# Key and value compression run as one pass: both halves of the array's columns, copies on ScalarE, sums shared with GpSimd

## The chip, the cores and the metric

The kernel runs on one core of a Trainium2 chip. The metric is the device time of one execution in microseconds (us), as the median of several runs. Engines are named as in the profile: PE (TensorE matmul), PEld (its weight load), DVE (VectorE), ACT (ScalarE), POOL (GpSimd), SP (SyncE, which issues the transfers).

## The reference

The program is a chain of blocks over 256 positions of width 1024: two "hybrid" layers, a gated delta-rule block with a context, and a mixture of 16 experts. The change is in the hybrid layers. Each projects its input to many streams, runs three attention mixers and mixes their results:

```python
h = split_cols(u @ w_in)                    # dq dk iq ik iw | fq fk fv | nq kc vc ks kw ... gate
o_dsa = dsa_mixer(dq, dk, h["dsa_v"], iq, ik, iw)   # top-64 keys by an index score
o_fox = fox_mixer(fq, fk, fv, logf)                 # six heads with a decay
kc = nsa_compress(kvs("nsa_kc"), cmp_pe[0], cmp_w1[0], cmp_w2[0])
vc = nsa_compress(kvs("nsa_vc"), cmp_pe[1], cmp_w1[1], cmp_w2[1])
...
def nsa_compress(kv, pe, w1, w2):           # 15 windows of 32 positions, stride 16, 2 groups of 64
    blocks = kv[:, idx] + pe                # idx: the 32 positions of each window
    return silu(blocks.reshape(..., 32 * 64) @ w1) @ w2
```

The nsa mixer, the third one, attends to the 15 compressed keys and values among others.

## The kernel before, in words

The two hybrid layers are two calls of `layer` (L661). It walks over a list of 17 chunks of the projection: NA, (dk, ik), (iq0, iq1), (dq0, dq1), (kc, vc), (fq0, fk0), NB, (fq1, fk1), and so on. A pair chunk has two halves of 128 columns. To keep fp32 precision, `halves` splits a half's weights into a rounded part `wh`, cast on ACT (L344), and the rest `wl = w - wh` (L345), on DVE or POOL by a pattern `self.pat`: "VVP" sends every third to POOL, "P" every one. `proj_t` then makes eight groups of three matmuls of a half (L433, L434 with `wh`, L435 with `wl`); the first L435 can't start before `wl` is there. NA, NB and NC use `proj_n` (L457) with two splits each. `w` loads of 1 MB are issued on SP.

The result of a half goes on in PSUM: `rope` (copy `rraw` on ACT, a rotation on PE, products on DVE L527 and POOL L528, sum L529) for dk, ik, iq, dq; a plain ACT copy for fq and fk; `compress` (L624) for kc and vc. When iq1 is there `topk` (L808) makes index scores `isc` (PE L819, ACT relu `irel`, DVE sums L829) and finds the 64th largest of each row with eight rounds of MAX8 and MATCH_REPLACE (L845, L846) on DVE, for 256 and for 128 columns, and from it the mask `dmask` (L850). dsa0, dsa1, fox0, ... are calls of `pair` (L532): masks and scores into PSUM on PE (dmask enters by L543, qk by L553), row maxima `nm` on DVE, exponentials on ACT, normalisation, transposes on PE (L592 to L594), PE products into O.

`compress` copies a half from PSUM to K2 (tile `sg`), 64 rows on ACT (L630) and the same shifted by one position into the other 64 rows on DVE (L631), for two groups; makes 16 tiles `cB` of 128x30 with the position's vector added (L634, DVE); multiplies them by `w1` into 64 rows of PSUM, accumulating over 16 (L637; two passes each, so 32 rows of the trace); and applies silu. Its `cB` has one buffer. `cmp_finish` (L872) multiplies by `w2` (L878, L887).

The order of instructions on each engine is not written out by hand: a scheduler orders the whole program when it is built, from dependences and buffers, so small edits move instructions of neighbouring work. In layer 1 a part of the third block, the context's chain, is put in beside the hybrid layer's chunks (`ctx_early`, L1280 to L1516: tiles yT, NB, NC, P, PT), and products of conditioning vectors (L372) fill gaps on PE. After the hybrid layers come the third block and the experts, whose weights (`rw`) stream through a ring of 21 tiles.

Of the kernel before, what the change touches and what calls it, by code (L numbers as in the profile page):

```python
# [186 lines left out]
def prep(inp):  # L187

    f = {k: np.asarray(v) for k, v in inp.items()}
    a = {}  # L190
    a["consts"] = CONST
    x = f["x"][0]
    a["xT"] = x.T.reshape(8, 128, 256).transpose(1, 0, 2)
    a["x"] = x
    a["cT"] = f["c"][0].reshape(8, 128).T

    slabs = lambda w: w.reshape(*w.shape[:-2], 4, 2, 128, 1024).swapaxes(-3, -2).reshape(*w.shape[:-2], 4, 128, 2048)

# [12 lines left out]
    a["cmp_pe"] = pe.reshape(2, 128, 32)
    w1 = f["cmp_w1"].reshape(2, 2, 16, 128, 64).transpose(0, 3, 1, 2, 4)
    a["cmp_w1"] = w1.reshape(2, 128, 2048)
    a["cmp_w2"] = f["cmp_w2"].transpose(0, 2, 1, 3).reshape(2, 64, 128)
    a["w_out"] = slabs(f["w_out"][:, MIX_ROWS, :])
    a["ln_g"] = f["ln_g"]
    a["ln_b"] = f["ln_b"]
    lc = np.stack([f["ln_g"], f["ln_b"]], 1).reshape(2, 2, 8, 128).transpose(0, 3, 1, 2)
    a["ln_col"] = lc.reshape(2, 128, 16)
    g = lambda n: f[n + "_2"]  # L220
    col = lambda v: v.reshape(8, 128).T
    a["c2T"] = np.concatenate([col(g("c")[0]), col(g("c_ctx"))], 1)
# [16 lines left out]
    a["w_gate"] = slabs(g("w_gate")[0])  # L239
    a["w_up"] = slabs(g("w_up")[0])  # L240
    a["w_down"] = slabs(g("w_down")[0][:15])

    a["w_down_last"] = strips(g("w_down")[0][15]).reshape(4, 128, 2, 1024).swapaxes(1, 2)
    a["fin_g"] = g("final_norm_g")[None]
    return {k: np.ascontiguousarray(v) for k, v in a.items()}


class Kern:
# [365 lines left out]
    def compress_consts(self, l):  # L614
        nc = self.nc
        w1 = self.wgtile().rearrange("p (a j o) -> p a j o", a=2, j=16)
        nc.sync.dma_start(w1, self.io["cmp_w1"][l].rearrange("p (a j o) -> p a j o", a=2, j=16))
        pe = self.t([128, 2, 16], "cpe", 2)
        nc.sync.dma_start(pe, self.io["cmp_pe"][l].rearrange("p (a j) -> p a j", a=2))
        w2 = self.t([64, 2, 64], "cw2", 2)  # L620
        nc.sync.dma_start(w2, self.io["cmp_w2"][l].rearrange("p (a o) -> p a o", a=2))
        return w1, pe, w2

    def compress(self, cc, a, p):  # L624

        nc = self.nc
        w1, pe, w2 = cc
        K2 = self.t([128, 2, 256], "sg", 1)
        for g in range(2):
            nc.scalar.copy(K2[0:64, g, :], p[64 * g:64 * g + 64, :])  # L630
            nc.vector.tensor_copy(K2[64:128, g, 0:255], p[64 * g:64 * g + 64, 1:256])  # L631
        B = self.t([128, 16, 2, 15], "cB", 1)
        for j in range(16):
            nc.vector.tensor_scalar(B[:, j], K2[:, :, 2 * j:2 * j + 225:16], pe[:, a, j:j + 1], None, op0=ALU.add)  # L634
        acc = self.psg([64, 2, 15])
        for j in range(16):
            nc.tensor.matmul(acc, w1[:, a, j, :], B[:, j], start=(j == 0), stop=(j == 15))  # L637
# [23 lines left out]
    def layer(self, l, uT, x, m, hook, first=None):  # L661
# [7 lines left out]
        for i, ch in enumerate(CHUNKS):  # L669
            if ch == ("kc", "vc"):  # L670
                cc = self.compress_consts(l)
            hook(i)
            self.pat = "P" if l == 0 and 3 <= i < 6 else "VVP"
            w = self.load_chunk(l, i) if l or i else first
            if isinstance(ch, str):
                N = self.t([128, 2, 256], ch)
                p = self.mmt()
                self.proj_n(p, w, uT)
                nc.vector.tensor_copy(N, p)
                S[ch] = N  # L680
                if ch == "NA":
                    self.after_na(N, bf, S)
                continue
            p = self.mmt()
            for ti, name in enumerate(ch):
                q = p[:, ti, :]
                self.proj_t(q, w[:, :, 128 * ti:128 * ti + 128], uT)
                if name[:2] in ("iq", "ik", "dk", "dq", "ks", "kw"):
                    S[name] = qk()
                    self.rope(S[name], q, 32 if name[0] == "i" else 64)  # L690
                elif name in ("kc", "vc"):
                    S[name] = self.compress(cc, 0 if name == "kc" else 1, q)
                elif name[0] == "g":
                    j = int(name[1])
                    e = self.t([128, 256], "ge", 2)
                    self.sigmoid_big(e, q)
                    nc.vector.tensor_mul(e, e, q)
                    g = S[f"mix{j}"]
                    nc.vector.tensor_mul(g, g, e)
                else:  # L700
                    S[name] = qk()
                    nc.scalar.copy(S[name], q)
                    if name[:2] == "nq":
                        S["r" + name] = qk()
# [1242 lines left out]
```

## Time and profile before

| | us |
|---|---|
| timed runs, median of 3 (lowest to highest) | 1303.93 (1303.80 to 1306.29) |
| the profiled execution's own time | 1295.95 |
| its span in the trace | 1294.2 |
| PE busy | 1048.7 (81%) |
| DVE busy | 558.6 (43%) |
| ACT busy | 387.4 (30%) |
| POOL busy | 264.6 (20%) |
| span of the chain that ended last spent in PE / DMA / DVE / POOL / ACT | 42% / 35% / 11% / 4% / 4% |

The profile lies 1.75 us around its span and 8 us below the timed median. Layer 0 takes about the first 240 us, layer 1 about 300 to 575 us, the experts the stretch from about 850 us on. A row of the timeline gives start, duration, engine, line, operation, what it writes and reads, and in brackets the idle time of its engine before it with what ended it.

### The profile page before, as it was taken

Reading aid. Unit: us, or ns where it says so; the run is one execution under the profiler, and the core shown is the slowest. Engines: PE = TensorE matmul, PEld = TensorE weight load, DVE = VectorE, ACT = ScalarE, POOL = GpSimd, SP = SyncE. Lnnn points to the kernel's source line nnn. Section 1 sums busy time; section 2 is a strip of 40 time slices with the busy share of each in tenths; the row PEclk is TensorE's granted clock in tenths of the full one; section 3 lists DMA queues with packets and bytes.
Section 4 is the critical chain, followed back from the end, with each engine's and each line's share of the span. In section 5 each row is a group of like instructions: output and inputs, shape, how many; then the busy total and the mean of one; then the engine's idle time right before and its main releaser. Section 6 shows DMA issues by size and latency. Waiting matters only on the chain.

```text
span 1294.2 us, 22853 instructions
## 1 busy us (share of the span) xinstructions
PE 1048.7 (81%) x9488; PEld 733.4 (57%) x9488; DVE 558.6 (43%) x1315; ACT 387.4 (30%) x899; POOL 264.6 (20%) x235
## 2 busy tenths in 40 slices
PE   5878999986869999957879999898666766676665
PEld 2766787776757876736778888654322432232232
DVE  2585357777696445586585435620100010010002
ACT  2334337635334425525542434310000000000002
POOL 1431132266421221152424343200000000000000
PEclk9899999999989999977979999899877787787777
DMA  8745864434224385521211555979999999999996
GB/s 357 263 160 204 311 228 171 140 130 176 102 88 168 140 305 191 215 78 39 95 58 40 192 202 215 363 288 417 421 420 419 421 419 420 419 420 420 420 421 247
DMA packets 52569, 330.07 MB, mean 255 GB/s; under 512 B 8049, under 2 KB 9969, under 8 KB 14321
## 3 DMA queue, kind: packets, MB, share of 16 engines
q1 hardware_dynamic: 52464, 328.61, 64.9%
q8 instruction: 74, 1.21, 0.4%
q14 instruction: 31, 0.25, 0.1%
HBM read 327.54 MB, written 1.05 MB: 254 GB/s over the span
## 4 chain that ended last, share of the span: by engine, by line
PE 42%; DMA 35%; DVE 11%; POOL 4%; ACT 4%; issue 4%; POOLq 0%; SPq 0%; DVEq 0%; ACTq 0%
DMA rw<-in_w_up 13%; DMA rw<-in_w_down 11%; DMA rw<-in_w_gate 5%; PE mm L433 4%; PE mm L435 4%; PE mm L434 4%; DMA w<-in_w_up 3%; PE s L476 3%; PE mm L457 3%; PE g L372 3%; DMA wg<-in_w_ada 3%; POOL wl L345 2%; PE s L1316 2%; ACT wh L344 2%; PE s L553 2%
## 5 line engine op out<-in xcount | busy, mean ns | idle before, releaser
L433 PE MATMUL mm<-uT,wh 128*128 128x256 f32 x576 | 173.1, 301 | 11.1 <-DVE yT L1247 6.6
L435 PE MATMUL mm<-uT,wl 128*128 128x256 f32 x576 | 167.7, 294 | 15.9 <-DVE wl L345 9.2
L344 ACT CAST wh<-w 128x1024 fp32r<-128x1024 f32 x124 | 127.6, 1033 | 154.1 <-PE mm L434 114.9
L434 PE MATMUL mm<-uT,wh 128*128 128x256 f32 x576 | 167.4, 291 | 0.0
L345 POOL TENSOR_TENSOR wl<-w,wh 128x1024 fp32r<-128x1024 f32 x47 | 114.2, 2431 | 200.3 <-ACT wh L344 168.1
L435 PEld LDWEIGHTS mm<-uT,wl 128*128 128x128 f32 x576 | 111.6, 195 | 25.9 <-DVE wl L345 10.1
L433 PEld LDWEIGHTS mm<-uT,wh 128*128 128x128 f32 x576 | 112.6, 196 | 22.7 <-issue 14.5
L1808 PE MATMUL g<-rw,XE 128*32 128x256 f32 x928 | 84.2, 469 | 41.3 <-DMA rw<-in_w_up 41.3
L345 DVE TENSOR_TENSOR wl<-w,wh 128x1024 fp32r<-128x1024 f32 x77 | 96.6, 1254 | 43.9 <-ACT wh L344 43.5
L434 PEld LDWEIGHTS mm<-uT,wh 128*128 128x128 f32 x576 | 112.4, 195 | 5.2 <-issue 4.0
L1808 PE MATMUL o<-rw,XE 128*32 128x256 f32 x944 | 85.3, 464 | 32.8 <-DMA rw<-in_w_gate 32.8
L1824 DVE TENSOR_TENSOR hd<-hd,g 128x256 f32<-128x256 f32 x16 | 6.7, 419 | 214.4 <-PE g L1808 214.4
L1820 ACT ACTIVATE hd<-o 128x256 f32<-128x256 f32 x16 | 6.1, 384 | 310.9 <-PE o L1808 310.9
L1852 PE MATMUL mm<-rw,hT 128*32 128x256 f32 x880 | 67.9, 446 | 18.7 <-DMA rw<-in_w_down 13.2
L1808 PEld LDWEIGHTS g<-rw,XE 128*32 128x32 f32 x928 | 31.8, 128 | 86.1 <-DMA rw<-in_w_up 66.8
L1808 PEld LDWEIGHTS o<-rw,XE 128*32 128x32 f32 x944 | 31.1, 125 | 76.8 <-DMA rw<-in_w_gate 53.9
L457 PE MATMUL mm<-wh,uT 128*128 128x256 f32 x256 | 54.0, 298 | 3.1 <-ACT wh L344 2.5
L1852 PEld LDWEIGHTS mm<-rw,hT 128*32 128x32 f32 x880 | 27.9, 124 | 49.5 <-DMA rw<-in_w_down 21.7
L457 PEld LDWEIGHTS mm<-wh,uT 128*128 128x128 f32 x256 | 41.6, 194 | 7.1 <-ACT wh L344 2.9
L565 ACT ACTIVATE P<-s,nm 128x256 f32<-128x256 f32 (+1 forms) x88 | 35.8, 419 | 18.9 <-DVE nm L558 18.7
L476 PE MATMUL s<-wh,m 128*128 128x512 f32 x128 | 41.2, 401 | 0.0
L457 PE MATMUL mm<-wl,uT 128*128 128x256 f32 x128 | 37.9, 296 | 0.8 <-DVE wl L345 0.7
(644 smaller groups left out, 1987.9 us busy)
## 6 DMA issues: line engine op xcount, KB each, us to landing
rw<-in_w_gate SPq DMA_DIRECT2D x59, 1024.0 KB, 19.9
rw<-in_w_up SPq DMA_DIRECT2D x58, 1024.0 KB, 19.9
rw<-in_w_down SPq DMA_DIRECT2D x55, 1024.0 KB, 19.8
w<-in_w_in SPq DMA_DIRECT2D x48, 1024.0 KB, 4.7
wg<-in_w_mod SPq DMA_DIRECT2D x24, 1024.0 KB, 4.9
wg<-in_w_ada SPq DMA_DIRECT2D x21, 1024.0 KB, 5.3
w<-in_w_out SPq DMA_DIRECT2D x12, 1024.0 KB, 4.8
w<-in_w_up SPq DMA_DIRECT2D x6, 1024.0 KB, 19.8
```

What stands on the lines that cost most here:

```text
L344: self.nc.scalar.copy(hi, w)
L345: self.lo_engine().tensor_sub(lo, w, hi)
L372: nc.tensor.matmul(p[32 * j:32 * j + 32, :], vec[:, 2 * q + kk, :], w[:, kk, 256 * j:256 * j + 256], start=(kk == 0 and (q == 0 or not who ...
L433: mm(out, wh[:, k, :], uh[:, k, :], start=(k == 0), stop=False)
L434: mm(out, wh[:, k, :], ul[:, k, :], start=False, stop=False)
L435: mm(out, wl[:, k, :], uh[:, k, :], start=False, stop=(k == 7))
L457: mm(p[:, tt, :], a[:, k, t], b[:, k % 4, :], start=(k == 0 and tt == 0 and j == 0), stop=(k == 7 and j == 2), skip_group_check=True)
L476: mm(Y(tt, n), a[:, t], b[:, 512 * n:512 * n + 512], start=(k2 == 0 and kk == 0 and i == 0), stop=(k2 == 3 and kk == 1 and i == 2))
L553: nc.tensor.matmul(S[:, h, o:o + n], qT[rows, t], kT[rows, :n], start=False, stop=True, skip_group_check=True)
L565: nc.scalar.activation(Pm[:, h, o:o + n], S[:, h, o:o + n], AF.Exp, bias=nm[:, i:i + 1], scale=0.125, accum_out=l[:, i:i + 1])
L1808: nc.tensor.matmul(pp[32 * j:32 * j + 32, :], XE[:, k, 32 * (e % 4):32 * (e % 4) + 32], w[:, kk, 256 * j:256 * j + 256], start=(k == 0), s ...
L1852: nc.tensor.matmul(py[32 * j:32 * j + 32, :], hT[:, cb, 32 * jj:32 * jj + 32], w[:, kk, 256 * j:256 * j + 256], start=(k == 0), stop=(k == 7))
```

## The change

Three things change. First, `compress` stops after the `cB` tiles: its shifted copy L631 is on ACT, `cB` has two buffers, and every fourth of the 16 sums is on POOL. Second, the multiplication by `w1` and the silu of keys and values are done together in `compress_both`, called from `cmp_finish`: the keys' matmuls write PSUM rows 0 to 63 and the values' rows 64 to 127, in turn, and one sigmoid serves 128 rows; `w2` is loaded as 128x64 to fit. Third, the pattern "P" for chunks 3 to 5, that is (dq0, dq1), (kc, vc) and (fq0, fk0), which held in layer 0 alone, holds in both layers.

```diff
-        w2 = self.t([64, 2, 64], "cw2", 2)
+        w2 = self.t([128, 64], "cw2", 2)
...
             nc.scalar.copy(K2[0:64, g, :], p[64 * g:64 * g + 64, :])
-            nc.vector.tensor_copy(K2[64:128, g, 0:255], p[64 * g:64 * g + 64, 1:256])
-        B = self.t([128, 16, 2, 15], "cB", 1)
+            nc.scalar.copy(K2[64:128, g, 0:255], p[64 * g:64 * g + 64, 1:256])
+        B = self.t([128, 16, 2, 15], "cB", 2)
         for j in range(16):
-            nc.vector.tensor_scalar(B[:, j], K2[:, :, 2 * j:2 * j + 225:16], pe[:, a, j:j + 1], None, op0=ALU.add)
-        acc = self.psg([64, 2, 15])
+            (nc.gpsimd if j % 4 == 3 else nc.vector).tensor_scalar(B[:, j], K2[:, :, 2 * j:2 * j + 225:16], pe[:, a, j:j + 1], None,
+                                                                   op0=ALU.add)
+        return B
+
+    def compress_both(self, cc, S):
+
+        nc = self.nc
+        w1, pe, w2 = cc
+        acc = self.psg([128, 2, 15])
         for j in range(16):
-            nc.tensor.matmul(acc, w1[:, a, j, :], B[:, j], start=(j == 0), stop=(j == 15))
-        s = self.t([64, 2, 16], "csil", 2)
+            for a, n in enumerate(("kc", "vc")):
+                nc.tensor.matmul(acc[HALF[a]], w1[:, a, j, :], S[n][:, j], start=(j == 0), stop=(j == 15))
+        s = self.t([128, 2, 16], "csil", 2)
...
-            self.pat = "P" if l == 0 and 3 <= i < 6 else "VVP"
+            self.pat = "P" if 3 <= i < 6 else "VVP"
...
+        s = self.compress_both(cc, S)
+        up, low = HALF
...
-            nc.tensor.matmul(p[64 * g:64 * g + 64, 0:16], w2[:, 0, :], S["kc"][:, g, :], start=True, stop=True)
+            nc.tensor.matmul(p[64 * g:64 * g + 64, 0:16], w2[up], s[up, g, :], start=True, stop=True)
```

Lines from L656 on have numbers higher by 8 in the changed kernel, and by 10 behind `cmp_finish`. Three places show how the orders move; all are in layer 1.

POOL, from the projection of ik to the context's first P: `wl` are lower halves, `qk` the rope's products, `foxl` the decay's rows. Before, the three rope products of ik, iq0 and iq1 stand in a row behind the lower half of iq1, and one lower half (kc) follows:

```order
L802 TENSOR_SCALAR foxl<-foxc,c_254 96x256 x3
L345 TENSOR_TENSOR wl<-w,wh 128x1024
L528 TENSOR_TENSOR qk<-rraw,c_254 128x256 x3
L345 TENSOR_TENSOR wl<-w,wh 128x1024
L528 TENSOR_TENSOR qk<-rraw,c_254 128x256
L834 TENSOR_SCALAR fm<-c_94 128x128
L528 TENSOR_TENSOR qk<-rraw,c_254 128x256
L1337 TENSOR_TENSOR P<-c_433,cgg 128x256
```

Now (after the same `foxl` and the lower half of iq1):

```order
L528 TENSOR_TENSOR qk<-rraw,c_254 128x256
L345 TENSOR_TENSOR wl<-w,wh 128x1024
L528 TENSOR_TENSOR qk<-rraw,c_254 128x256
L345 TENSOR_TENSOR wl<-w,wh 128x1024
L528 TENSOR_TENSOR qk<-rraw,c_254 128x256 x2
L345 TENSOR_TENSOR wl<-w,wh 128x1024
L842 TENSOR_SCALAR fm<-c_94 128x128
L345 TENSOR_TENSOR wl<-w,wh 128x1024
L528 TENSOR_TENSOR qk<-rraw,c_254 128x256
L345 TENSOR_TENSOR wl<-w,wh 128x1024
L634 TENSOR_SCALAR cB<-sg,cpe 128x30 x4
L345 TENSOR_TENSOR wl<-w,wh 128x1024
```

Lower halves of dq0 and dq1 now stand ahead of the rope products of iq0 and iq1, those of vc and fq0 behind kc's, then four sums for kc, and fk0's lower half ahead of the context's first P.

DVE, the last rounds of the smaller top-k up to its mask `dmask`. `ckr...` and `yT` belong to the context. Before:

```order
L631 COPY sg<-mm 64x255
L846 MATCH_REPLACE isc<-m_0_3535,isc 128x128
L417 TENSOR_SCALAR ckrqb<-ckrqb 128x8
L345 TENSOR_TENSOR wl<-w,wh 128x1024
L845 MAX m_0_3535<-isc 128x8
L418 TENSOR_TENSOR ckrs<-ckrqr,ckrqb 128x8
L631 COPY sg<-mm 64x255
L846 MATCH_REPLACE isc<-m_0_3535,isc 128x128
L1287 TENSOR_TENSOR yT<-s,ckrs 128x512
L850 SCALAR_TENSOR_TENSOR dmask<-isc,c_94 128x128
L1287 TENSOR_TENSOR yT<-s,ckrs 128x512
L634 TENSOR_SCALAR cB<-sg,cpe 128x30 x16
```

Now:

```order
L634 TENSOR_SCALAR cB<-sg,cpe 128x30
L853 MAX m_0_3526<-isc 128x8
L418 TENSOR_TENSOR ckrs<-ckrqr,ckrqb 128x8
L634 TENSOR_SCALAR cB<-sg,cpe 128x30
L854 MATCH_REPLACE isc<-m_0_3526,isc 128x128
L1297 TENSOR_TENSOR yT<-s,ckrs 128x512
L853 MAX m_0_3526<-isc 128x8
L1297 TENSOR_TENSOR yT<-s,ckrs 128x512
L854 MATCH_REPLACE isc<-m_0_3526,isc 128x128
L634 TENSOR_SCALAR cB<-sg,cpe 128x30
L858 SCALAR_TENSOR_TENSOR dmask<-isc,c_94 128x128
L634 TENSOR_SCALAR cB<-sg,cpe 128x30 x8
```

Between the last rounds there stand single sums `cB` in place of the two copies L631 and of one lower half (vc's); both products `yT` now stand ahead of `dmask`; the lower half that follows the sums is NB's, no more fq0's.

PE, the multiplication by `w1` (`cB` in the name), with NB's matmuls L457 around it. Before, a part of the values' run:

```order
L457 MATMUL mm<-wh,uT 128x256
L457 MATMUL mm<-wl,uT 128x256
L457 MATMUL mm<-wh,uT 128x256 x2
L457 MATMUL mm<-wl,uT 128x256
L637 MATMUL g<-cB,wg 64x30 x7
L457 MATMUL mm<-wh,uT 128x256
L637 MATMUL g<-cB,wg 64x30
L457 MATMUL mm<-wh,uT 128x256
L637 MATMUL g<-cB,wg 64x30 x2
L457 MATMUL mm<-wl,uT 128x256
L637 MATMUL g<-cB,wg 64x30
L457 MATMUL mm<-wh,uT 128x256
```

Now:

```order
L457 MATMUL mm<-wh,uT 128x256
L553 MATMUL s<-qk 128x256 x2
L553 MATMUL s<-qk 128x128 x2
L645 MATMUL g<-cB,wg 64x30 x32
L457 MATMUL mm<-wh,uT 128x256
L457 MATMUL mm<-wl,uT 128x256
L457 MATMUL mm<-wh,uT 128x256 x2
L457 MATMUL mm<-wl,uT 128x256
L457 MATMUL mm<-wh,uT 128x256 x2
```

The values' matmuls stood in eight pieces between NB's; keys' and values' now stand in one run of 32 instructions (64 passes), behind dsa1's scores.

## Rows read from the trace of the kernel before

**Rows 1.** The page: busy time of the engines; shares of the chain that ended last.

```profile
PE 1048.7 (81%) x9488; PEld 733.4 (57%) x9488; DVE 558.6 (43%) x1315; ACT 387.4 (30%) x899; POOL 264.6 (20%) x235
...
PE 42%; DMA 35%; DVE 11%; POOL 4%; ACT 4%; issue 4%; POOLq 0%; SPq 0%; DVEq 0%; ACTq 0%
```

**Rows 2.** Windows: stretch, length, busy PE, PEld, DVE, ACT, POOL; PEclk, DMA share, GB/s.

```profile
110.00:130.00 20.00, 20.00 (x169) 15.60 (x168) 10.87 (x41) 9.21 (x30) 2.59 (x5) 1.00 0.56 192
...
360.00:390.00 30.00, 19.63 (x174) 13.37 (x172) 26.65 (x99) 9.09 (x25) 6.72 (x8) 0.83 0.28 100
390.00:420.00 30.00, 28.67 (x231) 22.53 (x232) 20.56 (x76) 13.11 (x38) 3.50 (x3) 1.00 0.42 152
...
450.00:480.00 30.00, 30.00 (x285) 22.57 (x278) 14.60 (x40) 8.25 (x20) 10.56 (x9) 1.00 0.79 280
```

**Rows 3.** Windows: PE's longest pause in layer 1, and the stretch behind it.

```profile
361.50:369.60 8.10, 0.01 (x1) 0.00 (x0) 8.03 (x40) 1.45 (x5) 0.28 (x1) 0.67 0.00 0
369.60:374.20 4.60, 4.53 (x18) 3.81 (x18) 4.50 (x22) 0.59 (x1) 0.00 (x0) 0.50 0.00 0
```

**Rows 4.** Timeline of PE around that pause.

```profile
359.99 0.28 PE L434 MATMUL mm<-uT,wh 128*128 128x256 f32 x1
360.11 0.28 PE L435 MATMUL mm<-uT,wl 128*128 128x256 f32 x1
...
369.63 0.58 PE L435 MATMUL mm<-uT,wl 128*128 128x256 f32 x1 [8.11 <-DVE wl L345]
...
374.93 0.34 PE L543 MATMUL s<-dmask,bigI 128*128 128x384 bf16 x1
```

**Rows 5.** Timeline of DVE: end of layer 1's top-k.

```profile
367.63 0.42 DVE L631 COPY sg<-mm 64x255 f32<-64x255 f32 x1
...
368.36 1.22 DVE L345 TENSOR_TENSOR wl<-w,wh 128x1024 fp32r<-128x1024 f32 x1
...
370.65 0.69 DVE L1287 TENSOR_TENSOR yT<-s,ckrs 128x512 f32<-128x512 f32 x1
371.26 0.28 DVE L850 SCALAR_TENSOR_TENSOR dmask<-isc,c 128x128 bf16<-128x128 f32 x1
...
372.06 2.56 DVE L634 TENSOR_SCALAR cB<-sg,cpe 128x30 f32<-128x30 f32 x16
```

**Rows 6.** Timeline of POOL, then of ACT, in the same part.

```profile
344.38 1.50 POOL L528 TENSOR_TENSOR qk<-rraw,c 128x256 f32<-128x256 f32 x1 [4.49 <-ACT rraw L519]
350.86 2.56 POOL L345 TENSOR_TENSOR wl<-w,wh 128x1024 fp32r<-128x1024 f32 x1 [4.98 <-ACT wh L344]
...
355.32 0.30 POOL L834 TENSOR_SCALAR fm<-c 128x128 f32<-128x128 f32 x1 [1.04 <-DVE isc L835]
...
376.05 0.61 POOL L1337 TENSOR_TENSOR P<-c,cgg 128x256 f32<-128x256 f32 x1 [14.26 <-PE g L1341]
...
342.99 1.04 ACT L344 CAST wh<-w 128x1024 fp32r<-128x1024 f32 x1 [5.05 <-PE mm L434]
...
359.65 1.04 ACT L344 CAST wh<-w 128x1024 fp32r<-128x1024 f32 x1
```

**Rows 7.** Layer 0's top-k on DVE, with POOL's lower halves at that time.

```profile
75.59 2.00 DVE L829 SCALAR_TENSOR_TENSOR isc<-irel,iw,isc 128x128 f32<-128x128 f32 x1
...
78.60 0.33 DVE L829 SCALAR_TENSOR_TENSOR isc<-irel,iw,isc 128x128 f32<-128x128 f32 x1
...
81.87 0.61 DVE L845 MAX8 m<-isc 128x8 f32<-128x256 f32 x2
...
75.05 2.40 POOL L345 TENSOR_TENSOR wl<-w,wh 128x1024 fp32r<-128x1024 f32 x1
...
81.71 2.45 POOL L345 TENSOR_TENSOR wl<-w,wh 128x1024 fp32r<-128x1024 f32 x1
```

**Rows 8.** Timeline of PE: the compression's matmuls, layer 1.

```profile
399.70 2.05 PE L637 MATMUL g<-cB,wg 128*64 128x30 f32 x32
...
404.96 0.30 PE L637 MATMUL g<-cB,wg 128*64 128x30 f32 x2
```

More of the change, by code (lines that the diff above doesn't have):

```diff
@@ L213, in prep @@
     a["cmp_w1"] = w1.reshape(2, 128, 2048)
-    a["cmp_w2"] = f["cmp_w2"].transpose(0, 2, 1, 3).reshape(2, 64, 128)
+    a["cmp_w2"] = f["cmp_w2"].reshape(2, 128, 64)
     a["w_out"] = slabs(f["w_out"][:, MIX_ROWS, :])
@@ L619, in compress_consts @@
         nc.sync.dma_start(pe, self.io["cmp_pe"][l].rearrange("p (a j) -> p a j", a=2))
-        w2 = self.t([64, 2, 64], "cw2", 2)
-        nc.sync.dma_start(w2, self.io["cmp_w2"][l].rearrange("p (a o) -> p a o", a=2))
+        w2 = self.t([128, 64], "cw2", 2)
+        nc.sync.dma_start(w2, self.io["cmp_w2"][l])
         return w1, pe, w2
@@ L630, in compress @@
             nc.scalar.copy(K2[0:64, g, :], p[64 * g:64 * g + 64, :])
-            nc.vector.tensor_copy(K2[64:128, g, 0:255], p[64 * g:64 * g + 64, 1:256])
-        B = self.t([128, 16, 2, 15], "cB", 1)
+            nc.scalar.copy(K2[64:128, g, 0:255], p[64 * g:64 * g + 64, 1:256])
+        B = self.t([128, 16, 2, 15], "cB", 2)
         for j in range(16):
-            nc.vector.tensor_scalar(B[:, j], K2[:, :, 2 * j:2 * j + 225:16], pe[:, a, j:j + 1], None, op0=ALU.add)
-        acc = self.psg([64, 2, 15])
+            (nc.gpsimd if j % 4 == 3 else nc.vector).tensor_scalar(B[:, j], K2[:, :, 2 * j:2 * j + 225:16], pe[:, a, j:j + 1], None,
[5 more added lines that the diff above has]
+        acc = self.psg([128, 2, 15])
         for j in range(16):
-            nc.tensor.matmul(acc, w1[:, a, j, :], B[:, j], start=(j == 0), stop=(j == 15))
-        s = self.t([64, 2, 16], "csil", 2)
+            for a, n in enumerate(("kc", "vc")):
+                nc.tensor.matmul(acc[HALF[a]], w1[:, a, j, :], S[n][:, j], start=(j == 0), stop=(j == 15))
+        s = self.t([128, 2, 16], "csil", 2)
         nc.gpsimd.memset(s, 0.0)
-        th = self.t([64, 2, 15], "cth", 2)
+        th = self.t([128, 2, 15], "cth", 2)
         self.sigmoid(th, acc)
@@ L882, in cmp_finish @@
             nc.scalar.copy(S["kcT"][rows, 16 * g:16 * g + 16], p[rows, 0:16])
-        sr = self.t([64, 2, 3, 16], "csr")
-        nc.vector.tensor_copy(sr, S["vc"][:, :, None, :].to_broadcast([64, 2, 3, 16]))
+        sr = self.t([128, 2, 3, 16], "csr")[low]
+        nc.vector.tensor_copy(sr, s[low, :, None, :].to_broadcast([64, 2, 3, 16]))
         q = self.psg([96, 64])
-        nc.tensor.matmul(q, sr.rearrange("p a b c -> p (a b c)"), w2[:, 1, :], start=True, stop=True)
+        nc.tensor.matmul(q, sr.rearrange("p a b c -> p (a b c)"), w2[low], start=True, stop=True)
         vb = self.t([96, 6, 64], "vblk")
```

## The prediction

> **What bounds the kernel now.** I read the page first: PE is busy 81% of the span, and the chain that ended last lies 42% on PE and 35% on transfers [rows 1]. The transfers are the experts' weights at the end, which start when the earlier blocks are through, so what the hybrid layers gain or lose shifts the end by as much. The windows by stage come next. Around layer 0's compression PE is busy all 20 of 20 us; in layer 1 it is busy 28.67 and 30.00 of 30 us in the two later windows shown, but 19.63 of 30 from 360 to 390 us, where DVE is busy 26.65 and PE's granted clock is 0.83 [rows 2]. So PE sets the pace except in that one window, and there DVE does.
>
> The waits of PE in that window come down to one: from 361.5 to 369.6 us it does nothing, and then works 4.6 us at a granted clock of 0.50, the lower of its two levels (1.2 GHz) [rows 3]. It had stopped at vc's first L435, which waits 8.11 us for `wl` [rows 4]. The DVE timeline says why: that lower half takes 1.22 us, but stands at 368.36 among the top-k rounds [rows 5], though its `wh` was cast by 360.69. POOL idles 14.26 us up to 376.05 [rows 6]. The mask follows at 371.26, and PE takes it up only at 374.93 [rows 4, 5].
>
> **Lower halves to POOL in layer 1.** Four of six move to POOL: dq0, dq1, vc and fq0; iq1's and kc's are there already.
> - vc: cast done at 360.69, POOL free by then but for a rope product; 2.4 us [rows 7] make it ready at 363.1 to 363.8; I take 363.5. PE's stop ends 6.1 us earlier (369.6 less 363.5).
> - The slow stretch: 4.6 us at 0.50 did the work of 2.3 us at full clock. With a pause of 2 us in place of 8 I take the clock to stay up: 2.3 us more.
> - fq0 and fk0: POOL gives fq0's lower half at about 366.5 and, behind four sums and a wait for the cast, fk0's at about 371.4. PE's 24 matmuls of vc and of fq0 start 0.12 us apart at full clock [rows 4] and take some 2.9 us each, to 369.3: it waits 2.1 us for fk0. That is a cost.
> - dq0 and dq1: dq1's cast ends at 344.03, and its 2.4 us on POOL now stand ahead of iq1's rope product, which began at 344.38 and held 1.50 us [rows 6]. The index scores, and all of the top-k, start about 1.3 us later, kc's lower half some 2.2 us later (its L435 comes late enough to bear that).
>
> PE's account in layer 1 is thus -6.1 - 2.3 + 2.1 = -6.3 us, if the mask is not late. The mask: 371.26, plus 1.3 for the late start, less two copies and one lower half taken out of DVE's queue (0.42 + 0.42 + 1.22), plus four sums of 0.16 (2.56 over 16) and one `yT` of 0.69 that now stand ahead of it [rows 5]: 371.9. To this comes a price for POOL's company. In layer 0 a DVE sum of 0.33 us took 2.00 us while a lower half ran on POOL; a MAX8 beside another one took its usual 0.61 for two [rows 7]. So top-k proper is not held, but the small SBUF-to-SBUF operations between the rounds are, each until POOL's instruction ends. Per lower half that meets one, 0 to 2.1 us (2.4 less 0.33). I count one, fk0's, which is due at 369 to 371.4 among sums and the mask: 374.0. PE took the mask up at 374.93 before, and now has fk0's matmuls until about 374: no loss yet.
>
> The Trainium skill, "GPSIMD Engine Reference", section Specifications, says that GpSimd shares its SBUF interfaces with VectorE, and that they contend when DVE uses two SBUF inputs or a two-port mode. The trace agrees, with the 2.00 us [rows 7]; by that rule each of the four moved halves has its price on DVE, which is the second rival below.
>
> **Copies and sums.** Eight copies leave DVE (0.42 us each, [rows 5]) for ACT, whose nearest row, a cast of four times the columns, takes 1.04 [rows 6]; I count 0.4 each, and ACT is 30% busy [rows 1]. In layer 1 the four for vc wait for kc's last sum and stand ahead of copies of the context's chain, which waits for PE as well; I price this at 0 to +1, taking 0.5. The 16 sums on POOL have no row there; bounds are DVE's 0.16 and POOL's mask row of 0.30 [rows 6], so 0.6 to 1.2 us per four. One group of four stands between the context's P and PT, whose matmuls PE waits for: +1.
>
> **One pass of matmuls.** The first compression's 32 passes took 2.05 us in one run, 0.064 each; a piece of two between NB's matmuls took 0.30 [rows 8], 0.17 over its share. In layer 1 nine pieces (the keys' one and the values' eight) become one run: 8 x 0.17 = -1.4 us. Layer 0 had eight, two of keys and six of values, and now has two: 6 x 0.17 = -1.0. Both runs lie where PE is saturated [rows 2]. Whether matmuls on the two column halves run beside each other, no row shows: the gain is between 0 (64 passes of 0.064, 4.1 us as now) and half of it, 2.05 per layer. PE alternates between the halves at every instruction with a new weight load, so I take 0. It could also cost: the nearest row for switching is the 0.17 above, and 32 alternations at that price would be +5.4 a layer. The pieces differ in shape of array from their neighbours, while the halves are alike, so I set this end aside for the sum and keep it in the high end of the range.
>
> The Trainium skill, "TensorEngine Tiling (Array Packing)", section Key Properties, says that a change of tiling mode drains the engine, not a change of tile, and that tiles can load and multiply in parallel. The 0.30 us pieces agree with the first; the second is not shown here. By it the two layers would gain up to 4.1 us more.
>
> The shared silu saves a chain of five short instructions, which PE doesn't wait for: 0.
>
> **Layer 0.** Its lower halves were on POOL already. Two copies leave the queue ahead of its mask, and PE is saturated behind it: -0.5, between 0 and -2.
>
> **The sum.** -6.3 - 1.4 - 1.0 - 0.5 + 0.5 + 1 = -7.7. Because each engine's order is fixed when the program is built, some of the work that PE has done early leaves it without filler at a later softmax; 390 to 420 already holds 1.33 us of idling [rows 2], and I give back as much. The profiled execution's 1295.95 becomes 1289.6. The timed median is 8.0 above that execution; I carry the difference of -6.4 over: 1303.93 - 6.4 = 1297.5.
>
> **Rivals.**
> - *The gain is given back.* Layer 1's attention mixers follow one after another by softmaxes on DVE and ACT. If these and not PE's amount of work set 390 to 520, PE's lead turns into waits before later softmaxes, and only the pieces' 2.4 us and layer 0's 0.5 stay, less 1.5 for copies and sums: -1.4, 1302.5. For it: 1.33 us of idling in 390 to 420 at 95% busy. Against: 30.00 of 30 us in 450 to 480 [rows 2], so that filler is at hand.
> - *POOL's company holds DVE ahead of the mask.* If not one but four lower halves (dq1, vc, fq0, fk0) each meet a small DVE operation, three more stretches of 2.1 us put the mask at 374.0 + 6.3 = 380.3, some 5.4 after 374.93. PE runs out of matmuls at 374 and waits at lower clock, and dsa0 with everything behind it is 5.4 late. PE's lead (the work of 5 to 6 us) is then in vain where the softmaxes follow one another; with +1.5 for copies and sums and -2.9 for pieces and layer 0 it ends at +4.0: 1308. It decides from a mask later than about 377, which takes two such meetings more than I count. For it: 2.00 against 0.33 in layer 0, where the pattern is the same one [rows 7]. Against: MAX8 isn't held, and most of POOL's halves fall into MAX8 rounds.
> - *Halves run side by side.* Forecast less 4.1: 1293.4.
> - *The change doesn't do what it says:* vc's lower half on POOL is late because fm or the cast holds it. The order puts only `fm` (0.30) ahead of it, so I give this nothing of its own.
>
> **Chances and range.** Forecast as priced (1294.5 to 1301), 0.50; halves side by side or a full lead without any return (below 1294.5), 0.12; given back, 0.18; held by POOL, or the switching cost, 0.20. I call faster or slower what differs by over 0.2% (2.6 us), about what a measurement of this kernel can tell from no change. That gives 0.62 faster, 0.18 same, 0.20 slower. The range that leaves 1 in 10 on each side is 1290 to 1308; the likeliest case alone spans 1294.5 to 1301.
>
> **What would show it.** Right: vc's first L435 waits under 3 us; PE's busy time from 360 to 390 rises from 19.63 to about 26 with a clock near 1.0; `dmask` at 372 to 376; 64 compression passes in one row of about 4.1 us. Wrong: DVE rows of 2 us and more before `dmask` and L543 behind 378; compression passes far from 4.1 us; or a PE that idles in 390 to 520 for what it gained before.

## The result, and the profile after

| | before | after |
|---|---|---|
| timed, median (lowest to highest) of 4 runs | 1303.87 us (1302.89 to 1306.29) | 1289.1 us (1281.13 to 1289.93) |
| profiled execution, its span | 1295.95, 1294.2 us | 1289.07, 1287.3 us |
| PE, DVE, ACT, POOL busy | 1048.7, 558.6, 387.4, 264.6 us | 1049.1, 546.8, 389.6, 277.9 us |

The ratio is 0.987 (95% interval 0.9829 to 0.9911): faster, as forecast, but by 14.8 us and not 6.4, and 0.9 us below the range. For the experiments below the kernel before was run another 108 times, with a mean of 1300.0 us (standard deviation 4.9, from 1288.2 to 1311.0), and the changed one another 24 times, with a mean of 1289.6, and ratios of 0.9939 (0.9909 to 0.9969) and 0.9915 (0.9889 to 0.9941). So the gain is 10.4 us by the means; of the 14.8 some 4 us are where the first four runs of before happened to lie. The ratios leave out as slow four of these 108 runs, and one of the version with matmuls and sums, each over 1.5% above the fastest run beside it; without them the two means are 1299.7 and 1288.3, so that a difference from 1300.0 shrinks by 0.3 us.

A first view: windows of the changed kernel. The columns are those of [rows 2]; the first row has its counterpart of before behind it.

```profile
80.00:110.00 30.00, 26.75 (x215) 22.03 (x215) 23.70 (x92) 13.91 (x37) 11.69 (x13) 0.94 0.59 212
...
110.00:130.00 20.00, 19.62 (x217) 14.30 (x216) 8.71 (x22) 8.86 (x27) 4.04 (x4) 1.00 0.67 243
...
360.00:390.00 30.00, 22.47 (x198) 16.25 (x197) 26.18 (x87) 11.54 (x28) 10.84 (x15) 0.89 0.46 163
390.00:420.00 30.00, 29.91 (x265) 22.72 (x265) 16.81 (x51) 12.82 (x36) 3.86 (x4) 0.94 0.43 158
...
450.00:480.00 30.00, 28.93 (x262) 22.33 (x266) 15.64 (x45) 11.14 (x29) 6.44 (x6) 1.00 0.71 264
```

The same stretch, 80 to 110 us, before:

```profile
80.00:110.00 30.00, 22.28 (x176) 17.33 (x175) 23.24 (x87) 9.85 (x25) 8.11 (x5) 0.94 0.55 189
```

PE's idling in layer 0's mask and first attention falls from 7.72 to 3.25 us (in the second trace of before it is 6.31, in two more of the changed kernel 4.02 and 3.41). In layer 1 PE is busy 22.47 of 30 us where it was 19.63 [rows 2]. Layer 1 now begins 8.25 us earlier, as the marks below show, so the same work lies in windows that are earlier by 8.25 us:

```profile
351.75:381.75 30.00, 23.87 (x201) 19.22 (x199) 26.21 (x96) 13.05 (x34) 14.39 (x18) 0.89 0.26 92
381.75:411.75 30.00, 27.46 (x258) 20.45 (x258) 22.82 (x68) 11.74 (x36) 3.60 (x3) 0.94 0.56 208
...
441.75:471.75 30.00, 28.06 (x264) 22.66 (x263) 13.82 (x38) 6.94 (x16) 10.63 (x7) 1.00 0.81 298
```

That is 23.87 us for 19.63, less than the stop of 8 us and than the 26 of the forecast, at a granted clock of 0.89. Behind it PE idles more than before: 4.8 us in the three windows from 381.75 to 471.75, where the three from 390 to 480 of before held 1.6. The other traces of the two kernels, counted in the same way, have 4.5 and 4.8 against 1.7.

Where the time went is best read from three marks: the first DVE row that ends layer 0 and layer 1 (the residual sum `x<-x,z`, L743 before, L751 after) and a row late in the third block (L1591, L1601). Before:

```profile
267.36 0.69 DVE L743 SCALAR_TENSOR_TENSOR x<-x,z 128x512 f32<-128x512 f32 x1
...
560.70 0.69 DVE L743 SCALAR_TENSOR_TENSOR x<-x,z 128x512 f32<-128x512 f32 x1
...
776.61 1.29 DVE L1591 TENSOR_TENSOR uv<-uv,gvrs 128x512 f32<-128x512 f32 x2
```

After:

```profile
259.11 0.69 DVE L751 SCALAR_TENSOR_TENSOR x<-x,z 128x512 f32<-128x512 f32 x1
...
547.82 0.69 DVE L751 SCALAR_TENSOR_TENSOR x<-x,z 128x512 f32<-128x512 f32 x1
...
768.83 1.29 DVE L1601 TENSOR_TENSOR uv<-uv,gvrs 128x512 f32<-128x512 f32 x2
```

By these marks the layers of before end at 267 and 561 us, not at the rough 240 and 575 that were given ahead. Layer 0 ends 8.25 us earlier. Layer 1 takes 288.71 us where it took 293.34, 4.6 less. The third block, whose code the change doesn't touch, takes 221.01 where it took 215.91, 5.1 more. That pair of traces shows 6.9 us in all. The experiments say what each part owes to what.

What replaced the long pause in layer 1, on PE (timeline, as [rows 4]):

```profile
356.37 0.38 PE L435 MATMUL mm<-uT,wl 128*128 128x256 f32 x1 [1.08 <-POOL wl L345]
...
363.64 0.39 PE L433 MATMUL mm<-uT,wh 128*128 128x256 f32 x1 [1.79 <-ACT qk L710]
...
367.14 1.12 PE L1301 MATMUL g<-c,yT 128*128 128x128 f32 x4 [2.14 <-DVE yT L1297]
...
371.17 0.34 PE L543 MATMUL s<-dmask,bigI 128*128 128x384 bf16 x1
```

vc's L435 waits 1.08 us in place of 8.11. PE then waits for a buffer (`qk` on ACT) and for the context's `yT`, which DVE has late. The timeline of DVE in the changed kernel:

```profile
331.57 2.60 DVE L529 TENSOR_TENSOR qk<-qk,rtmp 128x256 f32<-128x256 f32 x1 [3.13 <-POOL qk L528]
...
346.41 2.46 DVE L843 TENSOR_TENSOR isc<-isc,fm 128x128 f32<-128x128 f32 x1
...
354.15 2.32 DVE L844 SCALAR_TENSOR_TENSOR isc<-c,isc 128x128 f32<-128x128 f32 x1
...
363.40 2.27 DVE L417 TENSOR_SCALAR ckrqb<-ckrqb 128x8 f32<-128x8 f32 x1
...
368.22 0.27 DVE L858 SCALAR_TENSOR_TENSOR dmask<-isc,c 128x128 bf16<-128x128 f32 x1
```

And that of POOL:

```profile
353.95 2.38 POOL L345 TENSOR_TENSOR wl<-w,wh 128x1024 fp32r<-128x1024 f32 x1 [4.52 <-ACT wh L344]
...
359.41 1.48 POOL L634 TENSOR_SCALAR cB<-sg,cpe 128x30 f32<-128x30 f32 x4
363.28 2.36 POOL L345 TENSOR_TENSOR wl<-w,wh 128x1024 fp32r<-128x1024 f32 x1 [2.38 <-ACT wh L344]
...
373.45 1.59 POOL L634 TENSOR_SCALAR cB<-sg,cpe 128x30 f32<-128x30 f32 x4
```

Four DVE operations on the way to the mask take 2.3 to 2.6 us, where their like take 0.16 to 0.43 alone, each until a lower half on POOL ends: L844 at 354.15 ends with vc's, L417 at 363.40, of 128x8 elements, with fk0's. Counted from the end of layer 0 the mask comes 5.2 us later than before (368.22 - 259.11 against 371.26 - 267.36), and PE takes it up 4.5 us later (371.17 - 259.11 against 374.93 - 267.36).

Layer 0's mask on DVE before, with the lower half that stood ahead of it:

```profile
90.07 1.21 DVE L345 TENSOR_TENSOR wl<-w,wh 128x1024 fp32r<-128x1024 f32 x1
...
93.31 0.29 DVE L850 SCALAR_TENSOR_TENSOR dmask<-isc,c 128x128 bf16<-128x128 f32 x1
```

After, where it stands behind:

```profile
91.28 0.29 DVE L858 SCALAR_TENSOR_TENSOR dmask<-isc,c 128x128 bf16<-128x128 f32 x1
...
92.73 1.22 DVE L345 TENSOR_TENSOR wl<-w,wh 128x1024 fp32r<-128x1024 f32 x1
```

The transposes (L592) of dsa0, dsa1 and fox0 then come 2.5, 3.0 and 6.7 us earlier. Before:

```profile
102.22 0.33 PE L592 MATMUL s<-c,P 128*128 128x128 f32 x1 [1.21 <-ACT P L578]
...
114.44 0.33 PE L592 MATMUL s<-c,P 128*128 128x128 f32 x1
...
129.65 0.33 PE L592 MATMUL s<-c,P 128*128 128x128 f32 x1
```

After:

```profile
99.70 0.33 PE L592 MATMUL s<-c,P 128*128 128x128 f32 x1 [1.19 <-ACT P L578]
...
111.45 0.27 PE L592 MATMUL s<-c,P 128*128 128x128 f32 x1
...
122.99 0.33 PE L592 MATMUL s<-c,P 128*128 128x128 f32 x1
```

The compression's matmuls stand between the transposes of dsa1 and of fox0, but the step from 3.0 to 6.7 isn't theirs alone. The transposes of fox0 with the copies alone, with the one pass of matmuls alone, and with both of these and nothing else (three of the versions below):

```profile
128.71 0.27 PE L592 MATMUL s<-c,P 128*128 128x128 f32 x1
...
125.71 0.27 PE L592 MATMUL s<-c,P 128*128 128x128 f32 x1
...
122.35 0.33 PE L592 MATMUL s<-c,P 128*128 128x128 f32 x1
```

They come 0.9, 3.9 and 7.3 us earlier than before: the two edits together give more than their sum. In the changed kernel NB's matmuls have also moved ahead of dsa1's transposes, which the scheduler did.

### The profile page after: what moved, and what is told of

Same layout as the page of the kernel before. It is cut to its first block, busy times and chain, and to the rows that moved or that the text cites. A ratio compares the mean times of both kernels' runs of the same rounds, so it can differ in the third digit from the quotient of the medians.

```text
span 1287.3 us, 22831 instructions
## 1 busy us (share of the span) xinstructions
PE 1049.1 (81%) x9488; PEld 739.2 (57%) x9488; DVE 546.8 (42%) x1279; ACT 389.6 (30%) x905; POOL 277.9 (22%) x253
## 3 DMA queue, kind: packets, MB, share of 16 engines
q8 instruction: 74, 1.21, 0.4%
## 4 chain that ended last, share of the span: by engine, by line
PE 39%; DMA 34%; DVE 11%; POOL 6%; ACT 5%; issue 4%; POOLq 0%; SPq 0%; DVEq 0%; ACTq 0%
DMA rw<-in_w_up 15%; DMA rw<-in_w_down 11%; DMA rw<-in_w_gate 5%; PE mm L433 4%; PE mm L435 4%; PE mm L434 4%; POOL wl L345 3%; PE s L476 3%; ACT wh L344 2%; PE mm L457 2%; PE s L1326 2%; PE g L372 2%; DMA wg<-in_w_ada 2%; PE o L582 2%; PE s L553 1%
## 5 line engine op out<-in xcount | busy, mean ns | idle before, releaser
L433 PE MATMUL mm<-uT,wh 128*128 128x256 f32 x576 | 174.9, 304 | 11.8 <-DVE yT L1257 6.6
L435 PE MATMUL mm<-uT,wl 128*128 128x256 f32 x576 | 168.8, 295 | 7.0 <-POOL wl L345 6.0
L345 POOL TENSOR_TENSOR wl<-w,wh 128x1024 fp32r<-128x1024 f32 x51 | 123.8, 2430 | 215.2 <-ACT wh L344 198.3
L434 PE MATMUL mm<-uT,wh 128*128 128x256 f32 x576 | 170.0, 295 | 0.0
L433 PEld LDWEIGHTS mm<-uT,wh 128*128 128x128 f32 x576 | 114.5, 199 | 23.2 <-issue 13.7
L435 PEld LDWEIGHTS mm<-uT,wl 128*128 128x128 f32 x576 | 113.9, 199 | 13.4 <-POOL wl L345 6.8
L434 PEld LDWEIGHTS mm<-uT,wh 128*128 128x128 f32 x576 | 114.8, 199 | 7.6 <-issue 6.8
L345 DVE TENSOR_TENSOR wl<-w,wh 128x1024 fp32r<-128x1024 f32 x73 | 89.8, 1230 | 45.9 <-ACT wh L344 45.6
L1862 PE MATMUL mm<-rw,hT 128*32 128x256 f32 x880 | 64.1, 426 | 24.0 <-DMA rw<-in_w_down 18.6
L457 PE MATMUL mm<-wh,uT 128*128 128x256 f32 x256 | 54.7, 302 | 3.1 <-ACT wh L344 2.5
L457 PEld LDWEIGHTS mm<-wh,uT 128*128 128x128 f32 x256 | 42.8, 199 | 7.8 <-issue 3.4
L457 PE MATMUL mm<-wl,uT 128*128 128x256 f32 x128 | 38.3, 299 | 0.7 <-DVE wl L345 0.7
```

The lines of the kernel that those rows point to most:

```text
L345: self.lo_engine().tensor_sub(lo, w, hi)
L433: mm(out, wh[:, k, :], uh[:, k, :], start=(k == 0), stop=False)
L434: mm(out, wh[:, k, :], ul[:, k, :], start=False, stop=False)
L435: mm(out, wl[:, k, :], uh[:, k, :], start=False, stop=(k == 7))
L457: mm(p[:, tt, :], a[:, k, t], b[:, k % 4, :], start=(k == 0 and tt == 0 and j == 0), stop=(k == 7 and j == 2), skip_group_check=True)
L1862: nc.tensor.matmul(py[32 * j:32 * j + 32, :], hT[:, cb, 32 * jj:32 * jj + 32], w[:, kk, 256 * j:256 * j + 256], start=(k == 0), stop=(k == 7))
```

## The experiments

All means are of the runs of one kernel, with their standard errors; "before" is its mean of 1300.0. They were timed on four chips, on each beside the kernel before, whose means there lie between 1299.8 and 1300.4.

**The pattern alone.**

```diff
-            self.pat = "P" if l == 0 and 3 <= i < 6 else "VVP"
+            self.pat = "P" if 3 <= i < 6 else "VVP"
```

> The kernel before with the pattern of the lower halves alone changed ("P" for chunks 3 to 5 in layer 1 too). Theory A (what the new trace suggests: most of the gain was made in layer 0, by the copies, the sums and the matmuls): 1 to 4 us faster than before. Theory B (the prediction's: PE's 8 us stop in layer 1 is the largest term): 5 to 7 us faster. In both vc's first L435 no longer waits 8 us.

1298.7 +- 1.3 in 12 runs; ratio 0.9997 (0.9967 to 1.0026): no change that can be told. In its trace vc's first L435 waits 0.98 us. Before, it waited 8.11, and 6.16 in the second trace of before. The rows of that trace and of this version, with this version's mask:

```profile
370.98 0.58 PE L435 MATMUL mm<-uT,wl 128*128 128x256 f32 x1 [6.16 <-DVE wl L345]
...
367.69 0.38 PE L435 MATMUL mm<-uT,wl 128*128 128x256 f32 x1 [0.98 <-POOL wl L345]
...
379.59 0.28 DVE L850 SCALAR_TENSOR_TENSOR dmask<-isc,c 128x128 bf16<-128x128 f32 x1
```

Layer 0 ends at 270.50 in this version, so its mask is 5.2 us late as in the changed kernel (109.09 behind that end against 103.90 before): the moved lower halves make it late, without any sum on POOL. Still layer 1 takes 288.1 us, 5.3 to 5.8 less than in the two traces of before, so the pattern is worth about what was priced there. Layer 0, whose code is the same, took 2.3 to 3.1 us more and the third block 221.2 us in that execution. The gain in its place is shown; that it reaches the end is not.

**The changed kernel with the old pattern** (that edit undone).

> The changed kernel with the old pattern in layer 1. Theory A: 9 to 13 us faster than before, since layer 0 is the changed kernel's. Theory B: 1 to 4 us faster than before.

1289.0 +- 1.1 in 10 runs, 0.9919 (0.9886 to 0.9951): theory A. The whole gain is there without the pattern.

**One pass of matmuls alone** (copies and sums on DVE, old pattern, two buffers of `cB`).

> The kernel before with the one pass of matmuls in both column halves and the second buffer of cB alone; copies and sums stay on DVE, the pattern is the old one. If the matmuls (fewer pieces, halves side by side) are the larger part of layer 0's gain: 5 to 8 us faster than before. If it is DVE's queue that the copies and sums relieve: 2 to 4 us faster.

1292.2 +- 0.9 in 12 runs, 0.9942 (0.9915 to 0.9969): 7.8 us, the upper end. The second buffer of `cB` and the shared silu go with the matmuls here; no run parts them.

Part of this gain was there to be read in the trace of before, among the pieces in layer 1:

```profile
404.65 0.38 PE L457 MATMUL mm<-wh,uT 128*128 128x256 f32 x1
404.96 0.30 PE L637 MATMUL g<-cB,wg 128*64 128x30 f32 x2
405.19 0.38 PE L457 MATMUL mm<-wh,uT 128*128 128x256 f32 x1
```

From the first start to the last are 0.54 us. One L457 takes 0.12 where they follow each other, and two passes 0.12 (0.058 each, below). So the piece costs about 0.30 us, not 0.17: the 0.30 of its own row leaves out the time that is lost ahead of it. As an estimate, 14 pieces fewer are worth 4.2 us, not 2.4.

**Keys first, then values**, in the changed kernel:

```diff
-        for j in range(16):
-            for a, n in enumerate(("kc", "vc")):
+        for a, n in enumerate(("kc", "vc")):
+            for j in range(16):
```

> The changed kernel with the 16 matmuls of the keys first and then the 16 of the values, in the same two column halves. If the halves run side by side because they alternate (64 passes in about 2.3 us), a run of 32 passes now takes about 2.0 us and the pair about 4.1 us, and the kernel is 3 to 4 us slower than the changed one. If the closer spacing has another cause, 64 passes stay near 2.3 us and the time stays the same.

1291.6 +- 0.5 in 12 runs, 0.9949 (0.9919 to 0.998), 2.0 +- 0.8 above the changed kernel's 1289.6 and less than the 3 to 4 expected. The row of 64 passes here (timeline of PE, layer 1):

```profile
400.55 3.71 PE L645 MATMUL g<-cB,wg 128*64 128x30 f32 x64
```

And in the changed kernel:

```profile
399.23 2.06 PE L645 MATMUL g<-cB,wg 128*64 128x30 f32 x64
```

It is the alternation, then, that brings a pass from 0.058 to 0.032 us, at a granted clock of 1.00 in both. That is 1.65 us a layer. In its one trace layer 1 takes 292.8 us, 3.9 to 4.6 more than in the changed kernel's three; the passes explain 1.65 of that, and the rest stays open.

**Copies and sums alone** (two separate compressions).

```diff
-            nc.vector.tensor_copy(K2[64:128, g, 0:255], p[64 * g:64 * g + 64, 1:256])
+            nc.scalar.copy(K2[64:128, g, 0:255], p[64 * g:64 * g + 64, 1:256])
-            nc.vector.tensor_scalar(B[:, j], ...
+            (nc.gpsimd if j % 4 == 3 else nc.vector).tensor_scalar(B[:, j], ...
```

> The kernel before with the shifted copies on ScalarE and every fourth sum on GpSimd alone; two separate compressions, one buffer of cB, old pattern. If the copies and sums by themselves relieve the mask's queue in layer 0: 2 to 4 us faster than before. If they only help where the matmuls are merged too (the keys' matmuls then wait for nothing that PE has to stand for): within 1.5 us of before.

1298.9 +- 0.9 in 12 runs, 0.9998 (0.9971 to 1.0025): the second.

**Copies alone** (the first pair of lines above).

> The kernel before with the shifted copies on ScalarE alone. In layer 0 PE's waits from 80 to 110 us should fall from 7.7 to about 4 us, as they did with copies and sums. If that gain of 3 to 4 us reaches the end: 1295 to 1297. If, without the merged matmuls, it is given back as with copies and sums together: 1298 to 1300.

1296.7 +- 0.7 in 12 runs, 0.9972 (0.9949 to 0.9996): 3.3 us. PE's idling from 80 to 110 us is 4.12 us (its window):

```profile
80.00:110.00 30.00, 25.88 (x205) 20.94 (x204) 22.48 (x83) 13.01 (x35) 8.84 (x5) 0.94 0.58 207
```

On its DVE timeline the mask is where the changed kernel has it:

```profile
91.23 0.29 DVE L850 SCALAR_TENSOR_TENSOR dmask<-isc,c 128x128 bf16<-128x128 f32 x1
```

**Matmuls and copies, sums on DVE, old pattern**, twice.

> One pass of matmuls and the copies on ScalarE; all sums on DVE, old pattern. Between the one with matmuls alone (mean 1292.2) and the one that has the sums on GpSimd too (1289.0). If the copies are what counts: 1288.5 to 1290. If the sums on GpSimd are: 1291.5 to 1293.

> The version with one pass of matmuls and the copies on ScalarE, sums on DVE and the old pattern, again. Its six runs had a mean of 1283.2 where before had 1299.9. If that holds: 1281 to 1286. If six runs drew a low level by chance: 1287 to 1291, as the one with the sums on GpSimd (1289.0).

1283.2 +- 1.8 and 1283.6 +- 1.6 in 6 runs each; 0.9883 (0.9839 to 0.9926) and 0.988 (0.9841 to 0.992). Neither forecast of the first was low enough, and the second came out at the level of the first: leaving the sums on DVE is worth 5.6 us against the version with the sums on POOL (1289.0).

**Matmuls and sums, copies on DVE, old pattern.**

> One pass of matmuls and every fourth sum on GpSimd; the copies stay on DVE, old pattern. Theory E: not faster than the matmuls alone (mean 1292.2), 1292 to 1295. If the sums help: 1288 to 1291.

1289.1 +- 1.8 in 12 runs, 0.9912 (0.9876 to 0.9947), from 1278.2 to 1297.4. The mean lies in the range of "the sums help", 3.1 +- 2.0 below the matmuls alone, and not in theory E's; the runs lie so far apart that this doesn't settle it.

**The changed kernel with all sums on DVE**, twice, and **the changed kernel again**, twice.

> The changed kernel with all sums back on DVE (its pattern, copies and matmuls kept). Theory E (the sums on GpSimd cost: four of them take 1.5 to 1.8 us there and hold a lower half or the context's P behind them): 4 to 6 us faster than the changed kernel, 1284 to 1287. Theory F (the pattern is what takes the gain of layer 1 away): like the changed kernel, 1289 to 1291.

> The changed kernel with all sums on DVE, again: 1282.5 to 1285.5 if the first six runs (mean 1284.0) told the level; 1288 to 1291 if they drew well and the sums' engine makes no difference. In its trace, the sum of slow stretches from 600 to 860 us should again be 41 us if that goes with the order of the kernel, and 24 or 31 us as likely if it is drawn anew by each execution.

> The changed kernel itself, beside the others on one chip. Theory A (the pattern in layer 1 is worth nothing to 2 us; matmuls, copies and sums make the gain): 1287 to 1290 us where the kernel before has a mean near 1300, as the changed kernel with the old pattern had (mean 1289.0). Theory B (the pattern adds its own gain to theirs): 1282 to 1285 us. Against the one with keys' matmuls before values' (mean 1291.6) it is 3 us faster if the side-by-side passes (1.65 us a layer by the two rows of 64 passes) reach the end.

> The changed kernel, in the same call as its versions: 1289 to 1292 as before (mean 1290.8), if the level belongs to the program.

Sums on DVE: 1284.0 +- 1.4 (6 runs) and 1285.0 +- 1.3 (12), together 1284.7. The changed kernel: 1290.8 +- 0.9 and 1288.5 +- 0.5 (12 each). That is the figure of theory E: with the sums on POOL the mean is 4.9 us higher (3.5 +- 1.4 between the two kernels that were timed on one chip). And with the sums on DVE the pattern makes no difference (1284.7 against 1283.4).

**Sums on POOL in one layer alone.**

```diff
-            (nc.gpsimd if j % 4 == 3 else nc.vector)
+            (nc.gpsimd if j % 4 == 3 and self.lay == 0 else nc.vector)      # or == 1
```

> The changed kernel with the sums on GpSimd in layer 0 alone (on DVE in layer 1). Theory E1 (the sums on GpSimd cost in layer 1, where POOL also has the four moved lower halves and the context's P and PT): 1283 to 1286, like the version with all sums on DVE (mean 1284.0). Theory E0 (they cost in layer 0): 1288 to 1291.

> The changed kernel with the sums on GpSimd in layer 1 alone. E1: 1288 to 1291, like the changed kernel (mean 1290.8). E0: 1283 to 1286.

Layer 0 alone: 1282.7 +- 0.7 in 6 runs, 0.9886 (0.9849 to 0.9923), the lowest mean of all versions, 17.3 us below before. Layer 1 alone: 1287.9 +- 0.9 in 12 runs, 0.9915 (0.9889 to 0.994). E1: the cost comes with the sums in layer 1. The reason that E1 gives, the moved lower halves beside them, isn't borne out: with the old pattern the sums cost 5.6 us too.

And by the traces the cost isn't paid in layer 1. Durations of the three parts from the marks above, trace by trace:

| trace | layer 0 | layer 1 | third block |
|---|---|---|---|
| before; again | 267.4; 268.2 | 293.3; 293.9 | 215.9; 219.1 |
| changed, three traces | 259.1; 263.1; 258.6 | 288.7; 288.9; 288.2 | 221.0; 221.1; 220.9 |
| sums on DVE, two traces | 259.4; 261.1 | 287.5; 289.8 | 221.4; 214.8 |
| sums on POOL in layer 0; in layer 1 | 258.5; 260.2 | 290.1; 289.2 | 214.8; 220.8 |
| old pattern; also sums on DVE (two) | 259.6; 258.3; 262.0 | 292.2; 290.8; 289.9 | 214.3; 214.5; 214.5 |
| matmuls alone; copies alone; pattern alone | 264.2; 263.9; 270.5 | 290.7; 291.1; 288.1 | 219.6; 220.9; 221.2 |
| copies and sums; matmuls and sums; keys first | 266.6; 260.3; 259.5 | 291.5; 290.1; 292.8 | 221.3; 216.1; 219.7 |

**A second trace of before.**

> A second trace of the kernel before. Theory C (the clock's slow stretches from 600 to 860 us, where all kernels run the same code, fall differently from run to run and make most of the spread of its times): the sum of stretches at the lower level between 600 and 860 us differs from the first trace's 30.6 us where its time differs from 1295.95, by about 1 us of time for 2 to 3 us of slow stretch. Rival D (they fall alike for one program, and the spread comes from the transfers at the end): the same 30.6 us, and the difference lies behind 860 us.

1301.37 us in its one run, 5.4 above the first trace, with 3.2 of them in the third block. The sum of slow stretches from 600 to 860 us (those at the lower level of the granted clock) is 42.2 us against 30.7: theory C. Sums on DVE shows both levels in one program, with 41.0 us of such stretches in its first trace and 20.5 in its second, so the level doesn't go with the order of the kernel. Windows 630 to 700 and 700 to 860 us of its first trace:

```profile
630.00:700.00 70.00, 59.11 (x568) 51.75 (x570) 47.01 (x97) 22.25 (x37) 23.68 (x23) 0.83 0.14 48
700.00:860.00 160.00, 149.00 (x1322) 123.06 (x1326) 74.35 (x142) 59.34 (x125) 43.94 (x36) 0.95 0.62 239
```

And of its second:

```profile
630.00:700.00 70.00, 56.95 (x616) 48.96 (x616) 47.62 (x100) 23.84 (x40) 26.50 (x27) 0.90 0.17 57
700.00:860.00 160.00, 148.69 (x1373) 121.42 (x1373) 74.32 (x142) 59.74 (x126) 43.73 (x35) 0.98 0.66 252
```

With a granted clock of 0.83 and 0.95 the block takes 221.4 us, with 0.90 and 0.98 it takes 214.8, at the same instructions. The changed kernel showed 0.83 and 0.95 in each of its three traces. Over all 18 traces the block takes 214.3 to 214.8 us where the slow stretches sum to 20.5 to 23.9, 215.9 and 216.1 where they sum to 30.7, and 219.1 to 221.4 where they sum to 41.0 to 42.2; copies and sums, 221.3 with 34.2, is the one that doesn't fit.

The timed runs fall apart in a like way. Of the 18 with all sums on DVE, 10 lie from 1278.2 to 1283.6 and 8 from 1286.9 to 1290.6; of the changed kernel's 24, none lies below 1286.4 (of its first four, one does, at 1281.1). So the 4.9 us look like a difference in how often an execution falls in the lower group, not like a cost of each one.

## Why the prediction was wrong, point by point

- **Layer 0** is the step that failed: "Two copies leave the queue ahead of its mask, and PE is saturated behind it: -0.5, between 0 and -2", with the pieces' -1.0. Measured: 8.25 us in the first pair of traces (4.3 to 9.7 over all pairs of the changed kernel's three and before's two); against the first trace of before the copies alone take 3.5 us off layer 0 and the matmuls alone 3.1. Three things were missed. A lower half of 1.21 us left the queue ahead of the mask as well, so the mask itself came 2.0 us earlier. PE was not saturated from 80 to 110 us: I read the window behind, 110 to 130 [rows 2], and not the one in which the mask falls; it idled there 7.72 us. And the alternating passes take little over half the time. The copies on ACT give the first two (shown by the copies alone: mask at 91.23, idling 4.1).
- **Halves side by side**: "I take 0" was wrong; the rival of 4.1 us was right in kind. In the row its size is right too: 64 passes take 2.06 us for the 4.1 of 64 at 0.064. Against the same run without alternation it is 1.65 a layer, and 2.0 +- 0.8 of time for both layers. The Trainium skill's statement in "TensorEngine Tiling (Array Packing)", Key Properties, that tiles load and multiply in parallel, agrees with 2.06 against 3.71 us.
- **One pass of matmuls**: priced -2.4, a term that was mis-sized: it took a piece's cost from the length of its row, 0.17, where the starts around it give 0.30. With -4.2 for the pieces and -3.3 for the halves the sum would be -7.5; alone it measured -7.8 +- 1.0. In its trace 3.1 us come in layer 0 and 2.6 in layer 1, against the first trace of before.
- **The pattern**: priced -6.3 on PE. In layer 1 its own trace shows -5.3 to -5.8, so the mechanism and the size are right. Of the whole change, layer 1's 4.6 us fit the 4.9 that were summed for it (-6.3 - 1.4 + 0.5 + 1 + 1.3), but by luck: the passes and pieces gave about 2.6 us more than priced, and PE's idling behind the mask grew by 3 us where 1.3 were allowed for, so the rival of the gain given back is true in part. And the end doesn't see the pattern: alone it is at 0.9997, and on top of the rest it gives nothing by the means.
- **POOL's company on DVE**: I counted one meeting more than before; there are three (with the lower halves of dq0, vc and fk0), of about 2.1 us each. That lies between the sum and the second rival: the mask is 5.2 us late, where the sum had 2.7 and the rival 9.0. Counted from layer 0's end of before, PE takes the mask up at 379.4, behind the 378 that was to show the forecast wrong. The rival's end did not follow: the lead of PE wasn't in vain, and layer 1 still became shorter. By the Trainium skill, "GPSIMD Engine Reference", Specifications, GpSimd contends with VectorE instructions that have two SBUF inputs or a two-port mode. The trace agrees for L843, a product of two SBUF tiles (2.46 us). L417 has one tile of 128x8 as input and was held too (2.27 us); whether it ran in a two-port mode, no row shows.
- **Sums on POOL**: priced +1, bounded by 0.30 a sum; four took 1.48 to 1.81 us, 0.37 to 0.45 each, above the bound. With copies and matmuls in place, their cost of about 5 us is shown by means and comes with layer 1's, but the traces don't show it in layer 1. Shown is that the third block's time goes with its slow stretches; that the sums decide how these fall is not. The block takes 219.7 to 221.1 us in the five traces with the pattern and sums on POOL in layer 1. But it takes 214.3 with the old pattern and such sums, and 219.6 and 220.9 in two kernels without either. Why stays open.
- **The comparison**: a mean of 1300.0 over 108 runs would have put the forecast at 1293.6, against 1289.6 in 24 runs. Right sign, and 6.4 for 10.4.

## What to carry to other kernels

Look for the waits of the critical engine in every copy of a repeated stage, not in the one with the longest pause: in the first pair of traces the same edit gained 8 us in layer 0, where no single wait from 80 to 110 us was above 3 us, and 5 in layer 1. Price a switch between kinds of matmul from start to start, not by the length of a row. Matmuls of 64 columns gained by alternating the two halves (0.032 us a pass for 0.058). Moving elementwise work to GpSimd was not free even where it was idle: VectorE operations of 0.16 to 0.43 us that met a lower half there took 2.3 to 2.6 us, until it ended (MAX8 kept its time [rows 7]).

## What the runs showed of the hardware that was not expected

The third block, with the same code, takes 214.3 to 221.4 us, in one and the same program too (221.4 and 214.8), and the granted clock of 630 to 700 us goes with it (0.83 against 0.90). Timed runs of one program spread over 5 to 23 us (before: 1288.2 to 1311.0), most of them over more than a single edit here is worth; the third block's 7 us are a part of that. A pair of traces can show 6.9 us where the means differ by 10.4. A sum of 128x30 elements takes 0.37 to 0.45 us on GpSimd and 0.16 in a row on VectorE.
